# The last norm of a two-layer decoder trunk: six squares summed in float32 and sent unsplit into the ones product, one output scaling on GpSimd, two between VectorE's additions

## The chip, the cores and the metric

One core of a Trainium2 chip runs the whole program. The time is device microseconds of one execution; a kernel's time is the median of its runs. Fewer is better. The engines are named as in the profile: PE (TensorE's products), PEld (its weight loads), DVE (VectorE), ACT (ScalarE), POOL (GpSimd), SP (the engine that issues nearly all DMAs).

## The reference

Two decoder layers on 528 tokens (16 meta tokens and 512 real ones), width 1024, then a final RMS norm, of which the 512 real tokens are kept:

```python
def rmsnorm(x, g):
    x32 = x.astype(jnp.float32)
    y = x32 * lax.rsqrt(jnp.mean(x32 * x32, axis=-1, keepdims=True) + EPS)
    return (y * g.astype(jnp.float32)).astype(x.dtype)
...
    ff = jax.nn.silu(jnp.einsum('bld,df->blf', hn, w_gate)) * jnp.einsum('bld,df->blf', hn, w_up)
    return h + jnp.einsum('blf,fd->bld', ff, w_down)
...
    for i in range(DEPTH):
        h = hybrid_layer(h, attn_norm[i], ...)
    h = rmsnorm(h, final_norm)
    return h[:, N_META:]
```

Everything is float32. What the change touches is the last line pair: the end of the second layer's feed-forward network and the final norm.

## The kernel before

The activations lie transposed in SBUF: eight tiles h0 to h7 of 128 features by 528 tokens. Products are made in the fp32r type: each operand is split into a high part (a cast on ScalarE) and a low part (a subtraction on VectorE), and three products stand for one in float32 (high x high, high x low, low x high). The feed-forward network runs in rounds of hidden blocks; its last round in the last layer is arranged for an early end of the final norm.

That last round works on the 512 real tokens in two halves: the first, A, has 272 tokens, the second, B, 240. For each half and each m from 0 to 7, `product` (L933) issues nine products into one PSUM bank, and `add_part` (L1126) adds the bank to h[m] on VectorE. All eight of A come first, then all eight of B. Behind the products of B for m = 0 to 7, Python functions `after_0` to `after_7` issue the norm's work, so their text sets the order in which most of it enters each engine's queue; calls marked `pin` keep their order.

For half A, `after_a` squares each h[m] on ScalarE (L1200), adds the squares on VectorE (L1202), and scales h[m] by the norm's weight on ScalarE into `th` (L1145). The sum is split into `sqh` and `sql`, and two products with a matrix of ones (`sums`, L1192) sum over the 128 partitions and spread the result. `root` (L1180) takes an approximate reciprocal square root on ScalarE, `newton` (L1184, L1186, L1188) refines it on VectorE. The result for A is `fin["ra"]`, in a tile named e in the profile. `out_a` (through `out`) multiplies two of the eight blocks of `th` by it in one 128x544 operation (L1168) and has SP issue their DMA to the output (L1171).

For half B, ScalarE squares h[m] (`square_b`, L1161). The first square is written to the accumulator `acc`, and VectorE adds four more to it (`sum_b`, L1164): five squares in all. The last three squares, of h5, h6 and h7, stay in tiles of their own, `fin["one"]`, and enter `sums` each as a float32 operand; `acc` enters split into `sqh` and `sql`, so five products in all. `acc`, the three squares, the root and Newton's scratch are parts of one tile named S in the profile. `scale_b` (L1149) scales by the norm's weight into `tl`, and `out_b` does what `out_a` does, four times on 128x480.

The functions that the change touches and what calls them:

Of the kernel before, what the change touches and what calls it, by code (L numbers as in the profile page):

```python
# [10 lines left out]
F32 = mybir.dt.float32  # L11
F32R = mybir.dt.float32r
# [4 lines left out]
NK = D // 128  # L17
# [23 lines left out]
def hybrid_kernel(ctx, tc, x_t, w_in, w_fl, w_out, w_gate, w_up, w_down, vecs, b_fg, rope, decay, mask, ident, out_t):  # L41
    nc = tc.nc
# [206 lines left out]
    def psum_a():  # L249
        return psa.tile([128, 512], F32, name="psa", tag="psa")  # L250
# [5 lines left out]
    def tt(name, dt=F32):  # L256
        tag, bufs = tags[name]
        return tmp.tile([128, T], dt, name=name, tag=tag, bufs=bufs)
# [4 lines left out]
    def fft(tag, dt=F32R, shape=(128, T), bufs=None):  # L263
        return phase["ffn"].tile(list(shape), dt, name=tag, tag=tag, bufs=bufs)
# [32 lines left out]
    def pin(f, pinned=True):  # L297
        if pinned:
            tc.keep_in_program_order(f)
# [546 lines left out]
    def ffn(l, st, real, last):  # L846
# [269 lines left out]
        else:  # L1116
# [4 lines left out]
            na, nb = PA[1] - PA[0], PB[1] - PB[0]  # L1121
            fin = {}
# [24 lines left out]
            def scale_b(*ms):  # L1147
                for m in ms:
                    pin(nc.scalar.activation(fin["yb"][:, m], h[m][:, cb], AF.Copy, scale=gf[:, m:m + 1]))  # L1149

            def square_b(m):
                if m == 0:
                    t = fft("S", F32, (128, 6, w), 2)
                    fin["one"] = [t[:, i, 0:nb] for i in range(3)]
                    fin["acc"], fin["rb"], fin["tb"] = (t[:, i, 0:nb] for i in range(3, 6))
                    d = fin["acc"]
                elif m < NK - 3:
                    fin["sq", m] = d = tt("sq")[:, 0:nb]
                else:
                    d = fin["one"][m - NK + 3]  # L1160
                pin(nc.scalar.activation(d, h[m][:, cb], AF.Square))  # L1161

            def sum_b(m):
                pin(nc.vector.tensor_add(fin["acc"], fin["acc"], fin["sq", m]))  # L1164

            def out(eng, y, r, k, c0, c1):
                pair = r.unsqueeze(1).broadcast_to([128, 2, c1 - c0])
                f = eng.tensor_mul(y, y, pair)  # L1168
                if eng is nc.vector:
                    pin(f)  # L1170
                nc.sync.dma_start(out_t[k:k + 2, :, c0 - META:c1 - META].rearrange("k p c -> p k c"), y)  # L1171

            def out_a(eng, k):
                out(eng, fin["ya"][k // HB][:, k % HB:k % HB + 2], fin["ra"], k, *PA)

            def out_b(eng, k):
                out(eng, fin["yb"][:, k:k + 2], fin["rb"], k, *PB)

            def root(r, v):
                pin(nc.scalar.activation(r, v, AF.Abs_reciprocal_sqrt, bias=epsc, scale=1.0 / D))  # L1180

            def newton(i, r, v, a):
                if i == 0:
                    pin(nc.vector.tensor_mul(a, r, r))  # L1184
                elif i == 1:
                    pin(nc.vector.scalar_tensor_tensor(a, v, D * EPS, a, ALU.add, ALU.mult))  # L1186
                else:
                    pin(nc.vector.scalar_tensor_tensor(r, a, 3.0 * D, r, ALU.subtract, ALU.mult))  # L1188

            def sums(v, parts):  # L1190
                for i, t in enumerate(parts):
                    nc.tensor.matmul(v, ones if t.dtype == F32R else ones.bitcast(F32), t, start=(i == 0), stop=(i == len(parts) - 1))  # L1192
# [15 lines left out]
            def after_0():  # L1208
                hi, lo, acc = fin["a"]
                pin(nc.vector.tensor_sub(lo, acc, hi.bitcast(F32)))  # L1210
                square_b(0)

            def after_1():
                square_b(1)

            def after_2():
                fin["va"] = psum_a()[:, 0:na]
                sums(fin["va"], fin["a"][0:2])
                fin["ra"], fin["ta"] = (fft("e", F32, (128, T), 2)[:, 0:na] for _ in range(2))
                root(fin["ra"], fin["va"])  # L1220
                sum_b(1)
                square_b(2)
                for i in range(3):
                    newton(i, fin["ra"], fin["va"], fin["ta"])

            def after_3():
                square_b(3)
                scale_b(0)

            def after_4():  # L1230
                sum_b(2)
                square_b(4)
                out_a(nc.vector, 0)
                scale_b(1)

            def after_5():
                sum_b(3)
                sum_b(4)
                square_b(5)
                fin["b"] = tt("sqh", F32R)[:, 0:nb], tt("sql", F32R)[:, 0:nb]  # L1240
                pin(nc.scalar.copy(fin["b"][0], fin["acc"]))
                scale_b(2)

            def after_6():
                square_b(6)

            def after_7():
                hi, lo = fin["b"]
                square_b(7)
                pin(nc.vector.tensor_sub(lo, fin["acc"], hi.bitcast(F32)))  # L1250
                v = psum_a()[:, 0:nb]
                sums(v, (hi, fin["one"][0], lo, fin["one"][1], fin["one"][2]))
                out_a(nc.vector, 2)
                out_a(nc.vector, 4)
                scale_b(3, 4)
                root(fin["rb"], v)
                scale_b(5, 6, 7)
                out_a(nc.vector, 6)
                for i in range(3):
                    newton(i, fin["rb"], v, fin["tb"])  # L1260
                for k in range(0, NK, 2):
                    out_b(nc.vector, k)

            end = NK * n
            places = [(end, after_a)] + [(end + n * (i + 1), f) for i, f in enumerate(
                (after_0, after_1, after_2, after_3, after_4, after_5, after_6, after_7))]
            steps += merge(rnd, places)
        for i in range(HB):
# [8 lines left out]
    def layer(l):  # L1277
# [87 lines left out]
        for g in range(2):  # L1365
# [15 lines left out]
                      ret_places(3, 52, 45.5, 47.5, 57.5, 55.5, 58.5, 60, 64.1, 63, 64.2))  # L1381
        plan += [op[3], op[7], op[11], op[15]] + op[16:]
        up = ffn(l, ff, real, real)
        plan += [lambda: enter("ffn"), start_ffn] + up
        return plan
# [77 lines left out]
```

## Time and profile before

| | us |
|---|---|
| median of 3 runs (lowest, highest) | 1263.06 (1262.17, 1263.28) |
| the profiled execution, its own time | 1261.7 |
| its span, first to last instruction | 1259.9 |
| PE busy in the span | 1249.5 |
| DVE, ACT, POOL busy | 992.2, 683.0, 264.8 |
| granted TensorE clock, mean | 0.999 |
| last nine-product group for h7 ends, first addition behind it starts | 1250.26, 1250.29 |
| last GpSimd operation before the change's place starts | 889.5 |

Times inside the execution count from the start of the span. A row of a timeline gives start, length, engine, line and operation, output tile <- input tiles, shapes, and a count where like rows are merged; the length is then from the first start to the last end, and successive operations of one engine overlap a little. In square brackets stands how long the engine was idle before and what ended that. An fp32r product is one record; a float32 product with the ones is two.

### The profile page before, as it was taken

The page shows a single profiled execution, that of the slowest core. Times are in us where ns is not written, and L with a number is a line of the kernel's source. Part 1 is how long each engine was busy: PE and PEld are TensorE (multiplying, and loading weights), DVE is VectorE, ACT ScalarE, POOL GpSimd, SP SyncE. Part 2 cuts the span into 40 slices and gives each one's busy share as a digit, 9 for nine tenths or more (in the row PEclk, how much of TensorE's full clock was granted, in tenths as well). Part 3 has the DMA queues.
Part 4 walks back from the last instruction along what each step waited for, and adds up shares of the span by engine and source line. Part 5 has one row for each costly group of instructions (what it writes and reads, how often), then busy time and mean ns, then how long its engine had stood idle before and what let it go on. Part 6 is the DMA issues. An engine that isn't in the chain of part 4 may idle for free.

```text
span 1259.9 us, 23793 instructions
## 1 busy us (share of the span) xinstructions
PE 1249.5 (99%) x9360; PEld 1192.6 (95%) x9360; DVE 992.2 (79%) x1851; ACT 683.0 (54%) x1239; POOL 264.8 (21%) x534
## 2 busy tenths in 40 slices
PE   9999999999999999999999999999999999999997
PEld 8999999999999999999999988998889999999996
DVE  8877856779888888887776777567899888888867
ACT  7666555776444444444455665457764444444445
POOL 3455645510000000000035545554100000000000
PEclk9999999999999999999999999999999999999999
DMA  7322223123333333332323222222323333333321
GB/s 237 86 76 90 80 77 93 51 74 124 93 98 101 99 101 101 101 101 84 102 77 118 76 94 78 90 78 67 109 86 124 101 101 101 101 101 101 100 84 68
DMA packets 45808, 120.58 MB, mean 96 GB/s; under 512 B 5488, under 2 KB 12400, under 8 KB 45696
## 3 DMA queue, kind: packets, MB, share of 16 engines
q1 hardware_dynamic: 45264, 118.77, 30.2%
q8 instruction: 73, 1.20, 0.4%
q14 instruction: 39, 0.32, 0.1%
q10 hardware_dynamic: 432, 0.29, 0.1%
HBM read 116.91 MB, written 2.13 MB: 94 GB/s over the span
## 4 chain that ended last, share of the span: by engine, by line
PE 98%; DVE 1%; DMA 1%; ACT 0%; SPq 0%; issue 0%; DVEq 0%
PE psd L207 32%; PE psa L933 19%; PE psd L1068 14%; PE psd L933 13%; PE psa L207 5%; PE psa L1068 4%; PE psa L438 2%; PE psa L615 2%; PE psa L528 2%; PE psa L782 1%; PE psa L752 1%; DMA h<-x_t 0%; PE psa L280 0%; PE psa L624 0%; PE psa L376 0%; DMA raw<-w_in 0%
## 5 line engine op out<-in xcount | busy, mean ns | idle before, releaser
L183 POOL TENSOR_TENSOR wlo<-raw,whi 128x128 fp32r<-128x128 f32 x504 | 259.4, 549 | 261.9 <-ACT whi L180 259.4
L207 PE MATMUL psd<-xh,whi 128*128 128x264 f32 (+1 forms) x792 | 195.6, 314 | 0.3 <-ACT xh L309 0.3
L207 PE MATMUL psd<-xh,wlo 128*128 128x264 f32 (+1 forms) x792 | 186.3, 303 | 0.0
L207 PE MATMUL psd<-xl,whi 128*128 128x264 f32 (+1 forms) x792 | 185.9, 302 | 0.3 <-DVE xl L310 0.3
L207 PEld LDWEIGHTS psd<-xh,whi 128*128 128x128 f32 x792 | 128.0, 189 | 5.3 <-ACT xh L309 0.8
L207 PEld LDWEIGHTS psd<-xh,wlo 128*128 128x128 f32 x792 | 126.8, 188 | 6.0
L207 PEld LDWEIGHTS psd<-xl,whi 128*128 128x128 f32 x792 | 127.3, 188 | 4.7 <-DVE xl L310 0.8
L180 ACT CAST whi<-raw 128x512 fp32r<-128x512 f32 (+1 forms) x167 | 98.1, 614 | 56.0 <-PE psd L207 37.9
L921 ACT CAST whi<-raw 128x1024 fp32r<-128x1024 f32 (+2 forms) x62 | 54.9, 885 | 53.0 <-PE psd L933 38.8
L921 ACT CAST fwhi<-raw 128x1024 fp32r<-128x1024 f32 (+2 forms) x62 | 55.6, 897 | 47.1 <-PE psd L933 39.6
L85 POOL MEMSET kl<- 64x528 f32 x2 | 1.1, 534 | 345.5 <-PE psa L933 345.4
L922 DVE TENSOR_TENSOR wlo<-raw,whi 128x1024 fp32r<-128x1024 f32 (+2 forms) x62 | 62.9, 1015 | 11.2 <-ACT whi L921 11.0
L922 DVE TENSOR_TENSOR fwlo<-raw,fwhi 128x1024 fp32r<-128x1024 f32 (+2 forms) x62 | 64.0, 1032 | 8.6 <-ACT fwhi L921 8.4
L933 PE MATMUL psa<-th,whi 128*128 128x264 f32 (+1 forms) x232 | 65.4, 282 | 0.0
L933 PE MATMUL psa<-th,wlo 128*128 128x264 f32 (+1 forms) x232 | 65.4, 282 | 0.0
L933 PE MATMUL psa<-tl,whi 128*128 128x264 f32 (+1 forms) x232 | 65.3, 282 | 0.0
L933 PE MATMUL psa<-th,fwhi 128*128 128x264 f32 (+1 forms) x224 | 63.4, 283 | 0.0
L933 PE MATMUL psa<-tl,fwhi 128*128 128x264 f32 (+1 forms) x224 | 63.3, 283 | 0.0
L933 PE MATMUL psa<-th,fwlo 128*128 128x264 f32 (+1 forms) x224 | 63.3, 282 | 0.0
L548 ACT ACTIVATE pd<-pd,nmax 128x144 f32<-128x144 f32 (+1 forms) x64 | 36.9, 576 | 42.0 <-DVE nmax L535 27.4
L921 ACT CAST fwhi<-S 128x1024 fp32r<-128x1024 f32 x20 | 21.0, 1050 | 70.3 <-PE psa L933 66.5
L999 ACT COPY e<-psa 128x264 f32<-128x264 f32 (+1 forms) x114 | 42.9, 376 | 28.3 <-PE psa L933 24.0
(352 smaller groups left out, 4008.3 us busy)
## 6 DMA issues: line engine op xcount, KB each, us to landing
raw<-w_in SPq DMA_DIRECT2D x54, 512.0 KB, 3.5
raw<-w_gate SPq DMA_DIRECT2D x44, 512.0 KB, 3.9
fraw<-w_up SPq DMA_DIRECT2D x38, 512.0 KB, 3.7
raw<-w_down SPq DMA_DIRECT2D x64, 256.0 KB, 2.8
raw<-w_out SPq DMA_DIRECT2D x16, 512.0 KB, 3.5
raw<-w_down SPq DMA_DIRECT2D x32, 192.0 KB, 2.5
bc<-cdr SPq DMA_DIRECT2D x16, 264.0 KB, 3.6
raw<-w_up SPq DMA_DIRECT2D x6, 512.0 KB, 3.4
```

The lines of the kernel that those rows point to most:

```text
L180: pin((nc.vector.tensor_copy if j + c0 == 0 else nc.scalar.copy)(hi, job["raw"][:, c0:c1]), pinned)
L183: pin(sub(lo[:, i:i + wide], job["raw"][:, c0 + i:c0 + i + wide], hi[:, i:i + wide].bitcast(F32)), pinned)
L207: nc.tensor.matmul(ps[1][b][:, 0:c1 - c0], w[:, wk, :], x[:, c0:c1], start=(k == 0 and i == 0), stop=(k == n - 1 and i == 2))
L438: nc.tensor.transpose(ps[:, 128 * j:128 * j + 128], src[:, o:o + 128], idt)
L528: nc.tensor.matmul(sc[0:nq, 0:c1 - c0], st["q"][s][:, q0:q0 + nq], kk[:, c0:c1], start=(i == 0), stop=(i == 1))
L548: nc.scalar.activation(pr, pr, AF.Exp, bias=nmax[0:nq], scale=-1.0, accum_out=rsum)
L615: nc.tensor.matmul(po[:, c0:SEQ], v[:, j, :], pp[:, j, META + c0:T], start=(j == 0 and i == 0), stop=(j == 4 and i == 1))
L921: nc.scalar.copy(hi, src)
L922: nc.vector.tensor_sub(lo, src, hi.bitcast(F32))
L933: nc.tensor.matmul(bank()[:, 0:b.shape[-1]], a[:, o + k, :], b, start=(fresh and k == 0 and i == 0), stop=(k == n - 1 and i == 2), skip_gr ...
L999: nc.scalar.copy(self.t["e"][:, i], self.t["x"][:, 0:w])
L1068: nc.tensor.matmul(v[:, 0:c1 - c0], a[:, s * n + k, :], b[:, c0:c1], start=(k == 0 and i == 0), stop=(k == n - 1 and i == 2))
```

## The change

The second half's accumulator takes six squares instead of five (h0 to h5); only those of h6 and h7 stay apart. It enters `sums` as it is, in float32, as the first of three operands. The scaling `out_a` of blocks 6 and 7 goes to GpSimd, issued in `after_3`; that of blocks 0 and 1 is issued in `after_3` too, that of blocks 2 and 3 in `after_5`, that of blocks 4 and 5 stays in `after_7`. One more of the `scale_b` calls stands behind `root`.

```diff
             def square_b(m):
                 if m == 0:
                     t = fft("S", F32, (128, 6, w), 2)
-                    fin["one"] = [t[:, i, 0:nb] for i in range(3)]
+                    fin["one"] = [t[:, i, 0:nb] for i in range(2)]
                     fin["acc"], fin["rb"], fin["tb"] = (t[:, i, 0:nb] for i in range(3, 6))
                     d = fin["acc"]
-                elif m < NK - 3:
+                elif m < NK - 2:
                     fin["sq", m] = d = tt("sq")[:, 0:nb]
                 else:
-                    d = fin["one"][m - NK + 3]
+                    d = fin["one"][m - NK + 2]
...
             def after_3():
                 square_b(3)
                 scale_b(0)
+                out_a(nc.gpsimd, 6)
+                out_a(nc.vector, 0)
 
             def after_4():
                 sum_b(2)
                 square_b(4)
-                out_a(nc.vector, 0)
+                sum_b(3)
                 scale_b(1)
 
             def after_5():
-                sum_b(3)
                 sum_b(4)
                 square_b(5)
-                fin["b"] = tt("sqh", F32R)[:, 0:nb], tt("sql", F32R)[:, 0:nb]
-                pin(nc.scalar.copy(fin["b"][0], fin["acc"]))
+                out_a(nc.vector, 2)
                 scale_b(2)
 
             def after_6():
                 square_b(6)
+                sum_b(5)
 
             def after_7():
-                hi, lo = fin["b"]
                 square_b(7)
-                pin(nc.vector.tensor_sub(lo, fin["acc"], hi.bitcast(F32)))
                 v = psum_a()[:, 0:nb]
-                sums(v, (hi, fin["one"][0], lo, fin["one"][1], fin["one"][2]))
-                out_a(nc.vector, 2)
+                sums(v, (fin["acc"], *fin["one"]))
                 out_a(nc.vector, 4)
-                scale_b(3, 4)
+                scale_b(3)
                 root(fin["rb"], v)
-                scale_b(5, 6, 7)
-                out_a(nc.vector, 6)
+                scale_b(4, 5, 6, 7)
```

On VectorE, from the end of half A's Newton steps to the first Newton step of half B (L1184); h_76 to h_80 are h3 to h7, th_15285 holds blocks 0 to 3 of half A and th_15286 blocks 4 to 7. Before:

```order
L1126 TENSOR_TENSOR h_76<-psa,h_76 128x240
L1126 TENSOR_TENSOR h_77<-psa,h_77 128x240
L1164 TENSOR_TENSOR S<-S,sq 128x240
L1168 TENSOR_TENSOR th_15285<-th_15285,e 128x544
L1126 TENSOR_TENSOR h_78<-psa,h_78 128x240
L1164 TENSOR_TENSOR S<-S,sq 128x240 x2
L1126 TENSOR_TENSOR h_79<-psa,h_79 128x240
L1126 TENSOR_TENSOR h_80<-psa,h_80 128x240
L1250 TENSOR_TENSOR sql<-S,sqh 128x240
L1168 TENSOR_TENSOR th_15285<-th_15285,e 128x544
L1168 TENSOR_TENSOR th_15286<-th_15286,e 128x544 x2
L1184 TENSOR_TENSOR S<-S 128x240
```

On the same engine and stretch, changed:

```order
L1126 TENSOR_TENSOR h_76<-psa,h_76 128x240
L1168 TENSOR_TENSOR th_15285<-th_15285,e 128x544
L1126 TENSOR_TENSOR h_77<-psa,h_77 128x240
L1164 TENSOR_TENSOR S<-S,sq 128x240 x2
L1126 TENSOR_TENSOR h_78<-psa,h_78 128x240
L1164 TENSOR_TENSOR S<-S,sq 128x240
L1168 TENSOR_TENSOR th_15285<-th_15285,e 128x544
L1126 TENSOR_TENSOR h_79<-psa,h_79 128x240
L1164 TENSOR_TENSOR S<-S,sq 128x240
L1126 TENSOR_TENSOR h_80<-psa,h_80 128x240
L1168 TENSOR_TENSOR th_15286<-th_15286,e 128x544
L1184 TENSOR_TENSOR S<-S 128x240
```

Two scalings and a fourth addition to S (`acc`) now stand between the additions to h, where one scaling and three additions stood, and one scaling is left behind that of h7.

On SP, at the end of its queue, behind the last weight loads (rows with + are new, with - gone):

```order
 L1048 DMA raw<-w_down 128x384 x8
+L1171 DMA out_t<-th_15286 128x2x272
 L1171 DMA out_t<-th_15285 128x2x272 x2
-L1171 DMA out_t<-th_15286 128x2x272 x2
+L1171 DMA out_t<-th_15286 128x2x272
 L1171 DMA out_t<-tl_15287 128x2x240 x4
```

The DMA of the blocks that GpSimd scales now heads the eight output DMAs.

On ScalarE, from the square of h4 (sq<-h_77) on:

```order
 L1161 ACTIVATE sq<-h_77 128x240
 L1149 ACTIVATE tl_15287<-h_74,gf 128x240
-L1161 ACTIVATE S<-h_78 128x240
-L1241 CAST sqh<-S 128x240
+L1161 ACTIVATE sq<-h_78 128x240
 L1149 ACTIVATE tl_15287<-h_75,gf 128x240
 L1161 ACTIVATE S<-h_79 128x240
 L1161 ACTIVATE S<-h_80 128x240
 L1149 ACTIVATE tl_15287<-h_76,gf 128x240
+L1180 ACTIVATE S<-psa,epsc 128x240
 L1149 ACTIVATE tl_15287<-h_77,gf 128x240
-L1180 ACTIVATE S<-psa,epsc 128x240
```

The cast is gone, the square of h5 goes to a tile of its own from which VectorE adds it, and the root stands one scaling earlier.

## The prediction

> **What bounds the kernel now.** I read the page first, then the chain of work that ended last, then the timeline of each engine over the last 15 us.
>
> ```profile
> span 1259.9 us, 23793 instructions
> PE 1249.5 (99%) x9360; PEld 1192.6 (95%) x9360; DVE 992.2 (79%) x1851; ACT 683.0 (54%) x1239; POOL 264.8 (21%) x534
> PE 98%; DVE 1%; DMA 1%; ACT 0%; SPq 0%; issue 0%; DVEq 0%
> ```
>
> TensorE carries 98% of the chain, and the edit touches none of its long products. What it can move is the last 1% or so, the chain behind the last product of the feed-forward network:
>
> ```profile
> 1245.21 5.06 PE psa L933 x45
> ...
> 1250.29 0.41 DVE h L1126
> 1250.70 0.32 DVE sql L1250
> 1251.01 1.91 DVE th L1168 x3
> 1252.92 0.33 DVE S L1184
> ...
> 1254.16 0.66 DVE tl L1168
> ...
> 1255.39 1.14 DVE tl L1168 x2
> ```
>
> So from 1250.29 the end waits on VectorE: the addition of h7, the split's rest, three scalings of the first token half, three Newton steps (from L1184), four scalings of the second half. The same stretch by engine, VectorE first, then ScalarE, TensorE and the output DMAs:
>
> ```profile
> 1246.72 0.44 DVE L1188 SCALAR_TENSOR_TENSOR e<-e 128x272 f32<-128x272 f32 x1
> 1247.08 0.72 DVE L1126 TENSOR_TENSOR h<-psa,h 128x240 f32<-128x240 f32 x2
> 1247.71 0.40 DVE L1164 TENSOR_TENSOR S<-S,sq 128x240 f32<-128x240 f32 x1
> 1248.03 0.72 DVE L1168 TENSOR_TENSOR th<-th,e 128x544 f32<-128x544 f32 x1
> 1248.66 0.40 DVE L1126 TENSOR_TENSOR h<-psa,h 128x240 f32<-128x240 f32 x1
> 1248.98 0.91 DVE L1164 TENSOR_TENSOR S<-S,sq 128x240 f32<-128x240 f32 x2
> 1249.81 0.89 DVE L1126 TENSOR_TENSOR h<-psa,h 128x240 f32<-128x240 f32 x2
> 1250.61 0.40 DVE L1250 TENSOR_TENSOR sql<-S,sqh 128x240 fp32r<-128x240 f32 x1
> 1250.93 1.99 DVE L1168 TENSOR_TENSOR th<-th,e 128x544 f32<-128x544 f32 x3
> 1252.84 0.40 DVE L1184 TENSOR_TENSOR S<-S 128x240 f32<-128x240 f32 x1
> 1254.16 2.37 DVE L1168 TENSOR_TENSOR tl<-tl,S 128x480 f32<-128x480 f32 x4
> ```
>
> ```profile
> 1249.93 0.39 ACT L1241 CAST sqh<-S 128x240 fp32r<-128x240 f32 x1 [0.42 <-DVE S L1164]
> 1250.62 0.68 ACT L1161 ACTIVATE S<-h 128x240 f32<-128x240 f32 x2
> 1251.21 0.86 ACT L1149 ACTIVATE tl<-h,gf 128x240 f32<-128x240 f32 x2
> 1252.30 0.46 ACT L1180 ACTIVATE S<-psa,epsc 128x240 f32<-128x240 f32 x1 [0.23 <-PE psa L1192]
> ```
>
> ```profile
> 1249.98 0.28 PE L933 MATMUL psa<-ah,fwlo 128*128 128x240 f32 x1
> 1250.37 0.38 PE L1192 MATMUL psa<-sqh,ones 128*128 128x240 f32 x1
> 1250.59 0.57 PE L1192 MATMUL psa<-S,ones 128*128 128x240 f32 x2
> 1251.07 0.38 PE L1192 MATMUL psa<-sql,ones 128*128 128x240 f32 x1
> 1251.29 0.97 PE L1192 MATMUL psa<-S,ones 128*128 128x240 f32 x4
> ```
>
> ```profile
> 1254.88 2.04 SPq L1171 DMA_DIRECT2D out_t<-tl  x4
> ```
>
> Two chains meet at the first Newton step, 1252.84. VectorE comes free from its third scaling then (1250.93 + 3 starts of 0.635; two of 0.635 and one of 0.72 make the 1.99). The root ends at 1252.30 + 0.46 = 1252.76. So VectorE's end of the scalings is late by only about 0.04 over the root: taking scalings away there buys 0.04 unless the root comes earlier too. From the first Newton step to the end everything is rigid (1.32 to the first scaling, 4 scalings 0.57 apart, DMAs), so the whole effect is the shift of that step.
>
> **The change, part by part.** Steps on VectorE, start to next start: 0.32 for a 240-wide addition (two in 0.72, each 0.40), 0.635 for a 544-wide scaling, 0.51 for an addition to `acc` right behind another one (two in 0.91).
>
> *Split removed.* ScalarE's cast (0.39) and VectorE's subtraction (a 0.32 step on the chain) go. On TensorE two products of 0.22 each go (1250.37 to 1250.59, 1251.07 to 1251.29). `acc` comes in as float32; such a product is two records about 0.20 apart (four in 0.97, the last 0.37), so 0.40. Sum: six records, 6 x 0.20, against 2 x 0.22 + 6 x 0.20. The wait for `sql`, 1250.99 to 1251.07, goes too.
>
> *A sixth square in the sum.* One float32 product less, but one more addition (0.32) on VectorE, ahead of h7's.
>
> *The scalings move.* One goes to GpSimd; the first goes one place up, ahead of h4's addition; the second (before, at 1250.93) now stands ahead of h6's addition, 0.635 more in front of h7. Behind h7 there is one scaling where a subtraction and three scalings stood.
>
> *Without GpSimd in the way*, the new VectorE queue starts: h3 1247.08, scaling 1247.40, h4 1248.03, sum 1248.35, sum 1248.86, h5 1249.18, sum 1249.50, scaling 1249.82, h6 1250.45, sum 1250.77, h7 1251.09 to 1251.50. TensorE finished h7's product at 1249.98 + 0.28 = 1250.26, so this addition is now 0.80 behind where it stood (1249.81 + 0.89 - 0.41 = 1250.29). Squares of h5 and h6 are ready in time (each 0.39, about 0.04 behind its addition). TensorE can start on `acc` 0.05 behind its last addition (as sqh's product at 1250.37 stood behind the cast's end, 1250.32), 1251.17 + 0.05 = 1251.22, and reach h7's pair at 1251.22 + 4 x 0.203 = 1252.03. h7's square ends at 1251.50 + 0.04 + 0.39 = 1251.93, so TensorE's own queue ends last: 1252.03 + 0.20 + 0.37 = 1252.60. Root from 1252.64 (0.04, as from 1252.26 to 1252.30) to 1253.10, first Newton step 1253.13. Against 1252.84: **+0.30**. VectorE's remaining scaling ends at 1251.41 + 0.72 = 1252.13 and covers nothing.
>
> *GpSimd in the way.* Its scaling (128x544, th and e, both in SBUF) is released by the same Newton end as VectorE's, 1246.72 + 0.44 = 1247.16. The trace has GpSimd in earlier stages:
>
> ```profile
> L183 POOL TENSOR_TENSOR wlo<-raw,whi x504: 445/462/1544, 19.6 to 889.5; 128x128 fp32r<-128x128 f32 x168
> L357 POOL MEMSET pth<- 128x768 f32 x2 | 1.5, 742 | 0.3 <-POOLq L1451 0.3
> 119.25 0.61 ACT L180 CAST whi<-raw 128x512 fp32r<-128x512 f32 x1
> 119.93 0.46 POOL L183 TENSOR_TENSOR wlo<-raw,whi 128x128 fp32r<-128x128 f32 x1 [2.00 <-ACT whi L180]
> 104.71 0.71 DVE L132 TENSOR_TENSOR rql<-tq,rqh 128x528 fp32r<-128x528 f32 x1 [0.23 <-ACT rqh L131]
> 111.27 1.02 DVE L132 TENSOR_TENSOR rkl<-tq,rkh 128x528 fp32r<-128x528 f32 x1 [0.28 <-ACT rkh L131]
> 110.85 0.88 POOL L183 TENSOR_TENSOR wlo<-raw,whi 128x128 fp32r<-128x128 f32 x2
> 111.27 1.34 POOL L183 TENSOR_TENSOR wlo<-raw,whi 128x128 fp32r<-128x128 f32 x2
> ```
>
> GpSimd starts about 0.07 behind its releaser (119.86 to 119.93). At 111.27 a GpSimd and a VectorE operation, both with two SBUF inputs, start together: VectorE's takes 1.02 where the same shape alone took 0.71, and the next GpSimd operation takes 1.34 - 0.42 = 0.92 instead of 0.46, until 0.32 behind VectorE's end (112.29 to 112.61). They don't share; one waits for the other. VectorE loses the other's remaining time less 0.15 (0.46 - 0.31). The Trainium skill, "SBUF — State Buffer", section "SBUF: two separate sides", says that GpSimd and a VectorE operation with two SBUF inputs lock a shared port pair, that the first to start has it for its whole instruction and that the other fully blocks. The trace agrees that one blocks, but VectorE comes in 0.15 before the end; by the rule's letter the sum below would be 0.30 + 1.40 - 0.16 = 1.54.
>
> In the new order GpSimd starts at about 1247.24 and VectorE's first scaling at 1247.40, so VectorE is the one that waits: delay = P - 0.16 - 0.15, P being GpSimd's duration. No row has P for 544 elements. Lower end: 0.46 for 128 and, for 416 more, no less than a memset's 742/768 = 0.97 ns each: 0.86. Upper end: the whole median row scaled, 0.462 x 544/128 = 1.96. In between, the 0.32 that GpSimd needs once VectorE is out of the way is at most 2.5 ns an element, so 0.14 + 544 x 2.5 ns = 1.50. That row is the nearest, being the same operation, and some of its 0.32 must be fixed, so I take 1.40. The Trainium skill, "GPSIMD Engine Reference", section "Elementwise — side-by-side cycle accounting", has about 2.6 cycles an element for two inputs at 1.2 GHz, which makes 0.46 + 416 x 2.17 ns = 1.36, an estimate; by it the sum would be 0.30 + 1.36 - 0.31 = 1.35.
>
> Delay 1.40 - 0.31 = 1.09, and nothing behind it has slack: all of VectorE's queue up to h7's addition follows back to back, so `acc`, the squares of h6 and h7, TensorE, the root and Newton shift by 1.09. First Newton step at 1254.22: 0.30 + 1.09 = **+1.4 us**. Bounds from P: 0.30 + 0.55 = 0.85, and 0.30 + 1.65 = 1.95.
>
> *What I cost at nothing.* h6's and h7's products need banks freed by the Newton step and h3's addition, both early, so TensorE doesn't stall. ScalarE has one more scaling behind the root, 4 x 0.385 after 1254.2, done by 1255.8; the third and fourth scaling of the second half need them at about 1256.7 and 1257.3. In SP's queue GpSimd's DMA now stands first: it waits until about 1248.7, and the next one's data come at 1249.2, so it holds nothing up; all first-half DMAs are out before the second half's (first at 1254.88 before, 1256.3 now). If GpSimd took 7 us that cover would be gone.
>
> The profiled execution took 1261.7, span 1259.9 plus 1.8 around it, 1.36 under the median of the runs, 1263.06. On its own time the sum is 1263.1; on the median **1264.5**, slower by 0.11%. About 0.2% (2.5 us) is what a measurement of this kernel can tell from no change, so my forecast is "within 0.2%".
>
> **Rivals.**
> *No blocking at the end* (GpSimd late, or the broadcast operand read otherwise): +0.30, 1263.4. The 0.31 at 111.27 speaks against it. If VectorE's scaling got in first, GpSimd would end at 1248.12 + 1.40 - 0.14 = 1249.38 and hold up the sum at 1248.35 by 1.03 - 0.15 = 0.88: about +1.2, which belongs to the forecast.
> *The chain really gets shorter.* If h7's addition stayed at 1250.29, the square, two products and root would put the first Newton step at 1252.3: -0.55, 1262.5, still within 0.2%. Against it: VectorE's queue has 0.96 more ahead of h7, where it waited only 0.16 for TensorE.
> *Slower beyond the bound.* One place: GpSimd's scaling holds VectorE longer. It decides from 0.30 + P - 0.31 = 2.53, P = 2.54: 4.7 ns an element, over the 3.6 of the whole median row; for it speaks that no row shows GpSimd reading a broadcast operand, and that one took 1.544 for 128. Time 1265.6 and more.
> *TensorE's clock falls in the new gap* (1250.26 to about 1252.3): six records of 0.20 at half speed, +1.2 on top, 1265.7.
>
> ```profile
> 1252.80:1259.90 7.10, 0.00 (x0) 0.00 (x0) 3.62 (x8) 1.11 (x3) 0.00 (x0) 0.81 0.73 249
> ```
>
> This row (length, busy times, granted clock 0.81) speaks against it: a mean of 0.81 over 7.1 us is half speed for 2.7 us, so the clock fell 4.9 us behind the last product, over twice the gap.
>
> **How the numbers follow.** Forecast (blocking, P 0.86 to 1.96) 0.76; no blocking 0.12; shorter chain 0.03; P over 2.5 0.06; clock 0.02; something unforeseen, faster, 0.01. So faster by over 0.2% 0.01, same 0.91, slower 0.08. The range runs from no blocking, 1263.4, to P = 1.96, 1265.0, widened by 0.5 for the scatter of the three runs (1262.17 to 1263.28): 1262.9 to 1265.5.
>
> **What the new profile would show.** Right: a POOL row of about 1.4 from 1247.24; VectorE's first 544-wide scaling at about 1.8 instead of 0.72; h7's addition near 1252.2; six records of S in the norm's products without a gap for `sql`; first Newton step near 1254.2, span near 1261.3. A first scaling of 0.72 makes it +0.3; a POOL row over 2.5 makes it slower than the bound.

## The result, and the profile after

| us | before | changed |
|---|---|---|
| median of 22 runs (lowest, highest) | 1262.74 (1262.01, 1263.83) | 1264.76 (1263.57, 1265.55) |
| profiled execution, span | 1259.9 | 1262.1 |

The ratio is 1.0014, 95% interval [1.0008, 1.0021]: slower by 2.0 us, of which the interval leaves 1.0 to 2.7. The ratio lies within the 0.2% of the prediction, the upper end of its interval just over. The lowest runs differ by 1.56, the highest by 1.72.

The timelines of the changed kernel, VectorE first, over the same place as before the change:

```profile
1247.37 0.44 DVE L1188 SCALAR_TENSOR_TENSOR e<-e 128x272 f32<-128x272 f32 x1
1247.73 0.40 DVE L1126 TENSOR_TENSOR h<-psa,h 128x240 f32<-128x240 f32 x1
1248.05 1.88 DVE L1168 TENSOR_TENSOR th<-th,e 128x544 f32<-128x544 f32 x1
1249.85 0.40 DVE L1126 TENSOR_TENSOR h<-psa,h 128x240 f32<-128x240 f32 x1
1250.17 0.90 DVE L1164 TENSOR_TENSOR S<-S,sq 128x240 f32<-128x240 f32 x2
1250.99 0.40 DVE L1126 TENSOR_TENSOR h<-psa,h 128x240 f32<-128x240 f32 x1
1251.31 0.40 DVE L1164 TENSOR_TENSOR S<-S,sq 128x240 f32<-128x240 f32 x1
1251.62 0.72 DVE L1168 TENSOR_TENSOR th<-th,e 128x544 f32<-128x544 f32 x1
1252.26 0.40 DVE L1126 TENSOR_TENSOR h<-psa,h 128x240 f32<-128x240 f32 x1
1252.58 0.40 DVE L1164 TENSOR_TENSOR S<-S,sq 128x240 f32<-128x240 f32 x1
1252.89 0.40 DVE L1126 TENSOR_TENSOR h<-psa,h 128x240 f32<-128x240 f32 x1
1253.21 0.71 DVE L1168 TENSOR_TENSOR th<-th,e 128x544 f32<-128x544 f32 x1
1255.04 0.41 DVE L1184 TENSOR_TENSOR S<-S 128x240 f32<-128x240 f32 x1 [1.12 <-ACT S L1180]
```

GpSimd, TensorE's last long product and the norm's products, the root:

```profile
1247.98 1.36 POOL L1168 TENSOR_TENSOR th<-th,e 128x544 f32<-128x544 f32 x1 [357.38 <-PE psa L933]
```

```profile
1250.63 0.28 PE L933 MATMUL psa<-ah,fwlo 128*128 128x240 f32 x1
1253.03 1.48 PE L1192 MATMUL psa<-S,ones 128*128 128x240 f32 x6 [2.12 <-DVE S L1164]
```

```profile
1254.55 0.46 ACT L1180 ACTIVATE S<-psa,epsc 128x240 f32<-128x240 f32 x1 [0.44 <-PE psa L1192]
```

One VectorE row stands out: the same 544-wide scaling takes 1.88 at 1248.05 and 0.72 at 1251.62. GpSimd's row lies beside the long one. VectorE's busy share counts the waiting as work, and the releaser named for GpSimd, a product 357 us earlier, isn't what it waited for last: it started 0.17 behind the Newton step (1247.37 + 0.44 = 1247.81), here and in every kernel below that has it. The chain of the changed kernel runs through VectorE, TensorE and the root:

```profile
1248.13 1.80 DVE th L1168
...
1252.26 0.40 DVE h L1126
1252.66 0.32 DVE S L1164
...
1253.03 1.50 PE psa L1192 x6
...
1254.55 0.47 ACT S L1180
```

To compare kernels I use one stretch from here on: from the end of the first half's last Newton step (L1188) to the start of the second half's first (L1184). Before: 1247.16 to 1252.84, 5.68 us. Changed: 1247.81 to 1255.04, 7.23. So the edit costs **1.55 us** in the trace. In all nine profiles TensorE's last long product ends 3.09 us behind the stretch's start, so nothing in these kernels holds TensorE up ahead of the norm. The two spans differ by 2.2, but 0.65 of that was there when the stretch began (1247.81 against 1247.16); it arose early, in code that the change doesn't touch: the first long product started at 6.02 instead of 5.31, and 0.64 was left of that lag, after some to and fro, at 51 us. The median's 2.0 against 1.55 is inside the interval; I don't explain the rest.

### The profile page after: what moved, and what is told of

It is laid out like the page before. It is cut to its first block, busy times and chain, and to the rows that moved or that the text cites. A ratio compares the mean times of both kernels' runs of the same rounds, so it can differ in the third digit from the quotient of the medians.

```text
span 1262.1 us, 23789 instructions
## 1 busy us (share of the span) xinstructions
PE 1249.3 (99%) x9358; PEld 1192.3 (94%) x9358; DVE 991.2 (79%) x1850; ACT 682.9 (54%) x1238; POOL 266.8 (21%) x535
## 4 chain that ended last, share of the span: by engine, by line
PE 96%; DVE 2%; DMA 1%; ACT 1%; issue 0%; DVEq 0%; ACTq 0%; SPq 0%
PE psd L207 31%; PE psa L933 18%; PE psd L1068 14%; PE psd L933 13%; PE psa L207 5%; PE psa L1068 4%; PE psa L438 2%; PE psa L615 2%; PE psa L528 2%; PE psa L782 1%; PE psa L752 1%; DMA h<-x_t 0%; PE psa L280 0%; PE psa L624 0%; DMA vec<-vecs 0%; PE psa L376 0%
```

## Experiments

Four of these kernels ran 10 or 11 times, and beside them the kernel before 33 times, with a median of 1262.88; the last three ran once each, and the kernel before once beside them, 1261.47. The whole time can't tell effects of under 1 us apart, so the stretch decides, and the whole times are given beside it.

**All four scalings on VectorE.** GpSimd's scaling moves to VectorE, behind the third.

```diff
                 scale_b(0)
-                out_a(nc.gpsimd, 6)
                 out_a(nc.vector, 0)
...
                 out_a(nc.vector, 4)
+                out_a(nc.vector, 6)
                 scale_b(3)
```

> The changed kernel, but the fourth scaling runs on VectorE behind the third; nothing on GpSimd at the end. Measured is the stretch from the end of the first half's last Newton step (L1188) to the start of the second half's first (L1184): 5.68 us before, 7.23 us changed. Theory (VectorE's first scaling is blocked by GpSimd's): that scaling is back at 0.72, the stretch loses the 1.16 us of blocking, 6.07, though VectorE has one scaling more, since it has that free while the root is awaited; the whole execution about 0.4 us over before. Rival (the longer VectorE queue ahead of h7 is what costs): the stretch stays at 7.2 or gains 0.6 for the fourth scaling, 7.8.

```profile
1248.00 0.44 DVE L1188 SCALAR_TENSOR_TENSOR e<-e 128x272 f32<-128x272 f32 x1
...
1248.68 0.72 DVE L1168 TENSOR_TENSOR th<-th,e 128x544 f32<-128x544 f32 x1
...
1252.36 0.40 DVE L1126 TENSOR_TENSOR h<-psa,h 128x240 f32<-128x240 f32 x1
1252.68 1.35 DVE L1168 TENSOR_TENSOR th<-th,e 128x544 f32<-128x544 f32 x2
1254.51 0.41 DVE L1184 TENSOR_TENSOR S<-S 128x240 f32<-128x240 f32 x1 [0.48 <-ACT S L1180]
```

The stretch is 6.07 (1248.44 to 1254.51): 1.16 less than in the changed kernel, which is what its first scaling had over 0.72. The fourth scaling is free: VectorE still waits 0.48 for the root. So in this order GpSimd took over work that costs nothing on VectorE. Median 1263.35, ratio to before 1.0005 [0.9996, 1.0014].

**GpSimd alone in the kernel before.**

```diff
                 square_b(3)
                 scale_b(0)
+                out_a(nc.gpsimd, 6)
...
-                out_a(nc.vector, 6)
```

> The kernel before with one edit: the scaling of blocks 6 and 7 goes to GpSimd, issued where the changed kernel issues it. Theory (blocking): the addition of h2's square, two inputs in SBUF, is the first VectorE operation to meet it and takes about 1.25 us instead of 0.40; additions with one input in PSUM are not slowed; the stretch goes from 5.68 to about 6.4. Rival (no blocking): the stretch is 5.64, since the root bounds it 0.04 us earlier.

```profile
1248.83 1.36 POOL L1168 TENSOR_TENSOR th<-th,e 128x544 f32<-128x544 f32 x1 [357.39 <-PE psa L933]
1248.90 0.40 DVE L1126 TENSOR_TENSOR h<-psa,h 128x240 f32<-128x240 f32 x1
1249.21 1.25 DVE L1164 TENSOR_TENSOR S<-S,sq 128x240 f32<-128x240 f32 x1
...
1255.03 0.41 DVE L1184 TENSOR_TENSOR S<-S 128x240 f32<-128x240 f32 x1 [0.56 <-ACT S L1180]
```

The 240-wide addition of a square, two inputs in SBUF, takes 1.25 instead of 0.40; h4's addition at 1248.90 runs beside GpSimd as well, has one input in PSUM, and stays at 0.40. The held-up addition reads neither `th` nor e, so it doesn't wait for a tile that the two operations share. Stretch 6.36, +0.69: of the 0.85 lost there h7's addition had 0.16 to spare, which it had waited for TensorE before. Median 1263.58, ratio 1.0005 [0.9996, 1.0015]. GpSimd's part lengthens the stretch in either order; the whole time of this kernel alone doesn't show it.

**The sum alone, six squares or five.** The first diff is against the changed kernel: its sum, with the scalings back on VectorE at their old places. The second is against the kernel before: its five squares, unsplit.

```diff
-                out_a(nc.gpsimd, 6)
-                out_a(nc.vector, 0)
...
+                out_a(nc.vector, 0)
                 sum_b(3)
...
-                out_a(nc.vector, 2)
                 scale_b(2)
...
+                out_a(nc.vector, 2)
                 out_a(nc.vector, 4)
...
+                out_a(nc.vector, 6)
```

```diff
-                fin["b"] = tt("sqh", F32R)[:, 0:nb], tt("sql", F32R)[:, 0:nb]
-                pin(nc.scalar.copy(fin["b"][0], fin["acc"]))
...
-                pin(nc.vector.tensor_sub(lo, fin["acc"], hi.bitcast(F32)))
...
-                sums(v, (hi, fin["one"][0], lo, fin["one"][1], fin["one"][2]))
+                sums(v, (fin["acc"], *fin["one"]))
```

> The changed sum alone: six squares added, unsplit in float32, three operands in the norm's products; all four scalings on VectorE at the places they had before. Theory: h7's addition moves 0.15 us, the split's step of 0.32 us behind it is gone, VectorE's three scalings still end last; stretch 5.5. Rival (the float32 sum or the sixth addition is what made the changed kernel slower): stretch over 5.9.

> The kernel before with one edit: the sum of five squares enters the norm's products in float32, unsplit; four operands, eight records. Theory: h7's addition stays where it was, the subtraction behind it (0.32 us) is gone, TensorE starts on the sum without a gap and ends about 0.4 us earlier; VectorE's three scalings still bound: stretch 5.36, 0.3 us less than before, too little for the whole time to show. Rival (TensorE's float32 passes bound instead): stretch 5.6 or more.

Both stretches are 5.35, 0.32 less than before: the subtraction's step on VectorE. Six squares:

```profile
1250.14 0.40 DVE L1164 TENSOR_TENSOR S<-S,sq 128x240 f32<-128x240 f32 x1
1250.50 0.41 DVE L1126 TENSOR_TENSOR h<-psa,h 128x240 f32<-128x240 f32 x1
1250.82 1.99 DVE L1168 TENSOR_TENSOR th<-th,e 128x544 f32<-128x544 f32 x3
1252.72 0.40 DVE L1184 TENSOR_TENSOR S<-S 128x240 f32<-128x240 f32 x1
```

Five squares, with TensorE's eight records in one run behind its last long product:

```profile
1250.21 1.78 PE L1192 MATMUL psa<-S,ones 128*128 128x240 f32 x8
1250.73 1.99 DVE L1168 TENSOR_TENSOR th<-th,e 128x544 f32<-128x544 f32 x3
1252.63 0.40 DVE L1184 TENSOR_TENSOR S<-S 128x240 f32<-128x240 f32 x1
```

I had 5.5 for six squares, since I let h7's addition slip by 0.15. It didn't: another operation stands between every two additions to `acc`, none of them takes the 0.51 step of one right behind another, and the addition of h7 still waits for TensorE. Medians 1262.16 and 1262.25, both ratios 0.9996, [0.9987, 1.0005] and [0.9988, 1.0005]: under before, not clear of it. If anything of this change is kept, it is one of these; in the stretch they are 1.87 us under the changed kernel.

**GpSimd's size.** GpSimd scales one block, VectorE the other, behind the last scaling.

```diff
-                out_a(nc.gpsimd, 6)
+                nc.gpsimd.tensor_mul(fin["ya"][1][:, 2], fin["ya"][1][:, 2], fin["ra"])
...
                 out_a(nc.vector, 4)
+                pin(nc.vector.tensor_mul(fin["ya"][1][:, 3], fin["ya"][1][:, 3], fin["ra"]))
+                nc.sync.dma_start(out_t[6:8, :, PA[0] - META:PA[1] - META].rearrange("k p c -> p k c"), fin["ya"][1][:, 2:4])
```

> The changed kernel with GpSimd scaling one block (128x272), VectorE the other behind the last scaling. Theory (blocking lasts as long as GpSimd's operation, which has a fixed part and about 2.2 ns an element): GpSimd takes 0.77 us, VectorE's first scaling 0.72 + 0.57 = 1.29 us instead of 1.88, stretch 6.64 against 7.23. Rivals: no fixed part, GpSimd 0.68 and the scaling 1.20; blocking that doesn't depend on the size, the scaling still 1.88.

```profile
1247.58 0.78 POOL L1229 TENSOR_TENSOR th<-th,e 128x272 f32<-128x272 f32 x1 [357.37 <-PE psa L933]
1247.65 1.29 DVE L1168 TENSOR_TENSOR th<-th,e 128x544 f32<-128x544 f32 x1
```

GpSimd's operation takes 0.78, VectorE's first scaling 1.29; the stretch is 6.64, the whole time 1262.91. Half the elements take 0.57 of the time, so there is a fixed part, and the blocking follows GpSimd's length.

**Who starts first.** VectorE's first scaling moves directly behind the Newton steps.

```diff
                 for i in range(3):
                     newton(i, fin["ra"], fin["va"], fin["ta"])
+                out_a(nc.vector, 0)
...
                 out_a(nc.gpsimd, 6)
-                out_a(nc.vector, 0)
```

> The changed kernel with VectorE's first scaling directly behind the Newton steps, ahead of h3's addition, so that it starts about 0.1 us before GpSimd's. Theory (whoever starts first has the way for its whole operation): VectorE's first scaling takes 0.72 us; GpSimd's takes about 1.8 us instead of 1.36; the block moves to the addition of h2's square, about 0.93 us instead of 0.40; stretch about 6.7. Rival (GpSimd always wins, or the two share): the first scaling takes over 1.2 us.

```profile
1247.09 0.72 DVE L1168 TENSOR_TENSOR th<-th,e 128x544 f32<-128x544 f32 x1
1248.36 0.93 DVE L1164 TENSOR_TENSOR S<-S,sq 128x240 f32<-128x240 f32 x1
1247.22 1.81 POOL L1168 TENSOR_TENSOR th<-th,e 128x544 f32<-128x544 f32 x1 [357.38 <-PE psa L933]
```

VectorE started 0.13 ahead: its scaling is at 0.72 and GpSimd takes 1.81. The wait moves to the next VectorE operation with two SBUF inputs, the addition of h2's square (0.93 instead of 0.40). Stretch 6.72, whole time 1262.63. The order decides who waits, not whether.

**Four pieces.** GpSimd's scaling is cut into four operations.

```diff
-                out_a(nc.gpsimd, 6)
+                hn = na // 2
+                for j in (2, 3):
+                    for s in (slice(0, hn), slice(hn, na)):
+                        y = fin["ya"][1][:, j, s]
+                        nc.gpsimd.tensor_mul(y, y, fin["ra"][:, s])
+                nc.sync.dma_start(out_t[6:8, :, PA[0] - META:PA[1] - META].rearrange("k p c -> p k c"), fin["ya"][1][:, 2:4])
```

> The changed kernel with GpSimd's scaling in four pieces of 128x136. Theory (blocking by single operations, PSUM additions leave gaps): each piece 0.48 us alone, VectorE's first scaling 1.0 us instead of 1.88, later pieces stretched while VectorE runs; the next additions with two SBUF inputs lose 0 to 0.15 us each; stretch about 6.5. Rival (GpSimd keeps its way until its queue is empty): first scaling about 2.3 us, stretch over 7.4.

```profile
1246.99 2.63 POOL L1233 TENSOR_TENSOR th<-th,e 128x136 f32<-128x136 f32 x4 [357.37 <-PE psa L933]
1247.06 0.99 DVE L1168 TENSOR_TENSOR th<-th,e 128x544 f32<-128x544 f32 x1
```

VectorE's scaling takes 0.99, so it gets in behind the first piece, and GpSimd's four pieces stretch to 2.63. Stretch 6.43, whole time 1262.11: the pieces give back 0.79 of the 1.16, but all on VectorE, 6.07, is still better.

## Why the prediction was right

*The price of GpSimd's scaling.* I took 1.40 between 0.86 and 1.96; it measured 1.36. With 272 elements at 0.775 and 136 at 0.479 (the first of the four pieces) the line is about 2.15 ns an element and 0.19 fixed. The estimate from the Trainium skill, "GPSIMD Engine Reference", section "Elementwise — side-by-side cycle accounting", was 1.36 too; the trace agrees.

*The blocking.* Predicted 1.09, measured 1.877 - 0.716 = 1.16; that it is VectorE's first scaling that waits, and for GpSimd, came as forecast. VectorE started 0.07 behind GpSimd, not 0.16, because GpSimd came 0.17 behind its releaser and not 0.07: the step "GpSimd starts about 0.07 behind" was taken from a wait for ScalarE's cast and didn't carry over. The 0.15 by which VectorE gets in ahead of GpSimd's end held: 0.13 (GpSimd's end at 1249.34 is 1.29 behind VectorE's start, the loss 1.16). By the letter of "whole instruction" in the Trainium skill ("SBUF — State Buffer", section "SBUF: two separate sides") the loss would be 1.29; in all five kernels with GpSimd it is 0.13 to 0.14 less.

*The queue without blocking.* Predicted +0.30; all scalings on VectorE gave 6.07 - 5.68 = +0.39. The 0.09 is TensorE's first product, here of the changed kernel (one record, then two together):

```profile
1253.03 0.47 PE L1192 MATMUL psa<-S,ones 128*128 128x240 f32 x1 [2.12 <-DVE S L1164]
1253.03 0.67 PE L1192 MATMUL psa<-S,ones 128*128 128x240 f32 x2 [2.12 <-DVE S L1164]
```

The first takes 0.47 and the next starts 0.31 behind it where the others stand 0.20 apart, in all six kernels in which TensorE waited for a float32 sum. In the five-square kernel, where it didn't wait, all eight take 0.37. My six records of 0.20 left that out; what makes it longer I didn't test.

*The sum.* 0.39 + 1.16 = 1.55, against 1.40. On the whole time 1264.76 against 1264.5, and that these lie so near is partly luck: the kernel before came out at 1262.74 and not at 1263.06, so the medians differ by 2.0 where I forecast 1.4.

*Costs of nothing.* They held: the products behind the first follow each other at 0.20, ScalarE's four scalings and SP's DMAs hold nothing up, and from the first Newton step to the span's end it is 7.06 against 7.08 before.

*The rivals.* No blocking is out (first scaling 1.88). The float32 sum makes nothing slower: alone it makes the chain shorter, by 0.32 of the 0.55 that I gave as the most. The clock rival didn't come true in any profile here (1.00 while the norm's products ran), but my argument against it was too strong. These rows, length first and the granted clock third from the end, are of the changed kernel:

```profile
1250.90:1254.50 3.60, 1.48 (x7) 1.03 (x6) 3.02 (x8) 2.21 (x6) 0.00 (x0) 1.00 0.50 175
1254.50:1262.10 7.60, 0.01 (x1) 0.00 (x0) 3.58 (x7) 2.00 (x5) 0.00 (x0) 0.55 0.48 166
```

From 1256 to 1259.6 the granted clock is 0.50. So 0.55 over 7.6 us is half speed for 6.8, and the clock fell at about 1255.3, 0.7 behind the norm's last product, where I had counted on 4.9.

## What to carry to other kernels

An engine that is free helps only if it takes work from the place where the end is decided, and if it doesn't stand in the way of the engine that decides: here GpSimd took a scaling that was hidden and held up VectorE for 1.16 us. Before an elementwise operation goes to GpSimd, look at which VectorE operations beside it have two inputs in SBUF, and count against the first of them what is left of GpSimd's operation when it starts, less 0.13 to 0.14 us. An addition with one input in PSUM wasn't held up. A queue in front of a result can be as dear as the chain behind it: ahead of h7's addition every step counted beyond the 0.16 us that it had to spare, behind it a scaling was free as long as the root was awaited.

## What the runs showed of the hardware

The clock's fall isn't tied to the last product. Over the nine profiles it came 3.7 us (five squares) to 8.1 us (GpSimd alone) behind the last long product, and 0.7 us (the changed kernel) to 5.3 us (GpSimd alone) behind the norm's last one. The traces record the full clock without a break for 1249.28 us in seven of the nine, in the changed kernel from 5.97 to 1255.25; it is 3.41 us more in the kernel before and 3.41 less with all scalings on VectorE. That fits a fall on a grid of 3.41 us counted from the rise, so that the time from the last product to the fall would be chance; no run here tests it. The longest gap ahead of the norm's products, 2.12 us in the changed kernel, was safe in its one profile; the others had at most 1.62. How long a gap is always safe stays open.

The clock's rise shows in the first long products: in the GpSimd-alone kernel they start 0.22 us apart until about 10.4 us, in the kernel before mostly 0.12 apart from about 6.5 on. The first of the two is 1.5 us behind the other at 51 us already, and as far behind at the stretch (1248.66 against 1247.16), though no code ahead of it differs. So part of the whole times' scatter is likely to come from there, and a stretch at the end leaves it out.
